# A hybrid encoder layer on one core: the DMA queue in the list scheduler's order, some products later, and fourteen products of a zero operand

## The chip, the cores and the metric

The kernel runs on one core of a Trainium2 chip. The metric is the device time of one execution in microseconds (us); runs of one kernel are summed up by their median. The engines of the core are TensorE (PE in the profile; its weight loads are PEld), VectorE (DVE), ScalarE (ACT), GpSimd (POOL) and SyncE (SP). All DMAs of this kernel are issued from SP's queue, one after the other.

## The reference, cut to what matters

One step of one layer, for 1024 frames of a new stream (prompt) and 32 frames of a running one (sample), with a width of 1024:

```python
h = rmsnorm(x, g_norm)
z = h @ w_in                      # 1024 x 8192: q, k, v of attention, q, k, v, gate of retention, two branch gates
o_a = DiffAttn(h)                 # 8 heads, two softmax maps each: p0 - lam * p1, chunk-causal; then rmsnorm
o_r = Retention(h)                # 8 heads, rotary, decay, a state carried from chunk to chunk; rmsnorm, swish gate
x = x + (sigmoid(g_a) * o_a + sigmoid(g_r) * o_r) @ w_o
x = x + (silu(rmsnorm(x) @ w_ff_gate) * (rmsnorm(x) @ w_ff_up)) @ w_ff_down      # 2816 wide
x = x + sigmoid(rmsnorm(x) @ w_ple_gate) * (p @ w_ple)
```

The sample's 32 frames attend to a cache of 512 keys and values. The new keys and values and the retention states are outputs too.

## The kernel before, in words

Every float32 operand of a large product is scaled and split into two 16-bit halves, and a product is made of three 16-bit ones (high by high, high by low, low by high). So each weight block is loaded in float32 into one of two staging buffers (1 MB each), squared and summed for its scale, and split by ScalarE (high half) and VectorE (low half).

**First stage (`stream`).** The frames are 9 tiles: 8 of 128 prompt frames and one of the 32 sample frames. For each of 8 heads, the tiles are projected one after the other (`project`, L860 to L862, and L871 for the sample tile), once for the attention columns (`unit_a`) and four steps later for the retention and gate columns (`unit_b`). The sample tile's projection is computed the other way around and brought back by `fold` (L878 to L889): ScalarE and VectorE add two parts into `suz`, and TensorE transposes it four times (L887). `attend` computes the scores (L1003 to L1006), the two exponentials, their weighted difference and its two halves (L1051); a DMA transposes the probabilities (L1056, `aT<-p`), and TensorE multiplies them with the values (L1064 to L1068). DMA transposes also bring q and k (L1193, L1195) and the mixed output (L1357) into the layout that TensorE needs; each is issued on SP. Around the last head come the mixed output's way back from memory (`last_mix`, L1464), the splits of `w_o`, the first output products for 352 frames (`wo_rows`, whose products are at L521 to L523) and the load of feed-forward block 0 (`load_gu(0)`, L566).

At the very start, `const_g` multiplies the norm gains onto all partitions (L706), `norm_x` normalizes a tile of x and transposes it on TensorE (L834), and `load_block_steps` loads and splits the first two weight blocks; `weight_scale` sums their squares over the partitions with one product (L336).

**Second stage (`stream_bc`).** The remaining output products, the feed-forward norm (`residual`, whose loads are L1706 and L1708), and 22 blocks of gate and up weights (`load_gu`, its scale's product in `weight_scale`, L336), each used by seven products of half the depth, in `gu_pair`. Then come the down products and the gated embedding, which no list orders.

**What sets the order.** A planner, `Flow`, runs Python generators. Each `yield` names an engine and an estimated time in us (`S`, `V`, `G`, `M` for ScalarE, VectorE, GpSimd and TensorE, `DM` and `X` for the one DMA queue, which it calls D), or a buffer to get and put, an event to wait for, or a delay. At each step it takes the generator that can start first, by its estimates and priorities, and the code behind that `yield` emits the instructions. For a load of 1 MB it estimates 2.9 us of D, for a transpose about 1.2 us, and a landing of 1.3 us and a little more (`landed`). A store is emitted some time after its data is there by the estimate: `store(..., 2.0)` for keys and values, `1.0` for the mixed output.

The instructions of the engines named in `manual_schedule` stay in the order in which they were emitted. Before, these are TensorE, VectorE, ScalarE and GpSimd; SP is not among them, and its DMAs are put in order by the framework's own scheduler:

```python
        with tc.manual_schedule(engines={mybir.EngineType.PE, mybir.EngineType.DVE, mybir.EngineType.Activation,
                                         mybir.EngineType.Pool}):
            flow.add(stream(), 3)
            flow.run()
```

An engine takes its instructions strictly in that order; one that waits holds all behind it.

## Time and profile before

| what | value |
|---|---|
| time, median of 3 runs | 1838.11 us (1836.81 to 1839.48) |
| the profiled execution's own time | 1843.89 us |
| its span, from the first to the last instruction | 1842.0 us |
| mean granted TensorE clock | 0.993 |
| bytes moved by DMA | 180.98 MB, 98 GB/s on the mean |
| DMA transposes issued | 4 x 72 |

In the profile, L12 is line 12 of the kernel. A group is written as line, engine, operation, output <- inputs. A row of the timeline has its start and duration in us from the span's start, and in brackets how long the engine was idle before it and what ended that. A row of windows has the stretch, its length, the busy time of each engine with its instructions, the granted TensorE clock (1.00 is full), the DMA engines' busy share and the rate in GB/s. A row of waits has the total in us, how often, and the longest.

### The profile page before, as it was taken

The numbers are of one execution on the slowest core, as the hardware profiler recorded it, in microseconds if no ns is written. First come the engines' busy times: TensorE is split into PE (matmuls) and PEld (weight loads), VectorE is DVE, ScalarE is ACT, GpSimd is POOL, SyncE is SP. The second block draws the span as 40 slices with busy tenths as digits, with TensorE's granted clock in tenths as the row PEclk, the third lists the DMA queues.
The fourth block names the chain that finished last, engine by engine and source line by source line (L and its number), as shares of the span: only waits on it lengthen the run. The fifth ranks groups of instructions, "written<-read, shape, count | busy, mean of one in ns | idle before, by whom it ended". The sixth has DMA issues, their size and how long they took to land. (4 is left out here: it accounts for less than half of the span.)

```text
span 1842.0 us, 37081 instructions
## 1 busy us (share of the span) xinstructions
PE 1793.9 (97%) x13391; PEld 1154.5 (63%) x13391; DVE 1455.6 (79%) x3881; ACT 1063.9 (58%) x2750; POOL 617.3 (34%) x1038
## 2 busy tenths in 40 slices
PE   7899999999999999999999999999999999999999
PEld 3455555555555555555556867777777766666666
DVE  7888788788787887878886889999999967544553
ACT  7677777677777777777554445655555522102421
POOL 3654546454554655545530002323232100000110
PEclk9999999999999999999999999999999999999999
DMA  6354433445444444434357203221211163121111
GB/s 201 104 125 102 114 86 98 100 104 112 90 109 109 101 123 87 125 82 121 84 155 239 91 5 105 82 93 59 70 47 57 45 263 104 69 78 47 51 48 44
DMA packets 235563, 180.98 MB, mean 98 GB/s; under 512 B 187345, under 2 KB 217553, under 8 KB 227186
## 3 DMA queue, kind: packets, MB, share of 16 engines
q1 hardware_dynamic: 235378, 178.61, 34.3%
q8 instruction: 105, 1.72, 0.4%
q14 instruction: 80, 0.66, 0.1%
HBM read 112.34 MB, written 27.02 MB: 76 GB/s over the span
## 5 line engine op out<-in xcount | busy, mean ns | idle before, releaser
L860 PE MATMUL pj<-w,xh 128*128 128x512 f16 x1024 | 390.3, 381 | 3.1 <-ACT w L512 1.7
L861 PE MATMUL pj<-w,xh 128*128 128x512 f16 x1024 | 390.2, 381 | 0.8 <-DVE w L514 0.8
L862 PE MATMUL pj<-w,xh 128*128 128x512 f16 x1024 | 390.0, 381 | 0.0
L521 PE MATMUL ps<-xh,w 128*128 128x352 f16 (+1 forms) x1000 | 272.9, 278 | 2.2 <-DVE xr L1432 1.9
L523 PE MATMUL ps<-xh,w 128*128 128x352 f16 (+1 forms) x1000 | 272.8, 278 | 1.4 <-DVE w L549 1.4
L522 PE MATMUL ps<-xh,w 128*128 128x352 f16 (+1 forms) x1000 | 272.8, 278 | 0.9 <-DVE xh L1597 0.9
L523 PEld LDWEIGHTS <-w 128*128 128x128 f16 x1632 | 160.2, 98 | 54.1 <-issue 5.4
L521 PEld LDWEIGHTS <-w 128*128 128x128 f16 x1632 | 160.3, 98 | 48.8 <-issue 1.5
L522 PEld LDWEIGHTS <-w 128*128 128x128 f16 x1632 | 160.2, 98 | 48.8 <-issue 2.3
L862 PEld LDWEIGHTS <-xh 128*128 128x128 f16 x1024 | 100.5, 98 | 123.4 <-issue 3.8
L860 PEld LDWEIGHTS <-xh 128*128 128x128 f16 x1024 | 101.0, 99 | 89.2 <-issue 2.2
L861 PEld LDWEIGHTS <-xh 128*128 128x128 f16 x1024 | 100.6, 98 | 85.3 <-issue 4.0
L558 POOL TENSOR_TENSOR st<-st 128x512 f32<-128x512 f32 x54 | 72.0, 1334 | 237.3 <-DVE w L549 174.2
L522 PE MATMUL ps<-tT,w 128*128 128x352 f16 (+1 forms) x504 | 137.3, 277 | 3.2 <-DVE tT L1597 3.2
L523 PE MATMUL ps<-tT,w 128*128 128x352 f16 (+1 forms) x504 | 137.3, 277 | 0.0
L521 PE MATMUL ps<-tT,w 128*128 128x352 f16 (+1 forms) x504 | 137.3, 277 | 0.0
L1023 ACT ACTIVATE p<-sc,nb,scs 128x256 f32<-128x256 f32 (+7 forms) x128 | 106.1, 830 | 50.4 <-DVE nb L1015 37.2
L549 DVE SCALAR_TENSOR_TENSOR w<-st,gus,w 128x512 f16<-128x512 f32 x126 | 128.2, 1020 | 0.1
L1013 DVE TENSOR_REDUCE nm<-sc 128x1 f32<-128x640 f32 (+6 forms) x112 | 102.8, 918 | 25.8 <-PE sc L1006 24.2
L1573 PE MATMUL ps<-a,w 128*128 128x352 f16 x312 | 97.5, 313 | 0.5 <-DVE w L1778 0.5
L1572 PE MATMUL ps<-a,w 128*128 128x352 f16 x312 | 97.5, 312 | 0.0
L1571 PE MATMUL ps<-a,w 128*128 128x352 f16 x312 | 97.5, 312 | 0.0
(439 smaller groups left out, 4588.5 us busy)
## 6 DMA issues: line engine op xcount, KB each, us to landing
st<-in_win_dram SPq DMA_DIRECT2D x30, 1024.0 KB, 5.3
st<-in_wgu_dram SPq DMA_DIRECT2D x22, 1024.0 KB, 5.0
st<-in_wdn_dram SPq DMA_DIRECT2D x16, 704.0 KB, 4.1
out_dram<-kv SPq DMA_DIRECT2D x64, 128.0 KB, 1.9
a_d<-a SPq DMA_DIRECT2D x9, 528.0 KB, 2.7
b<-a_d SPq DMA_DIRECT2D x9, 528.0 KB, 6.8
xh<-mix_d SPq DMA_DIRECT2D x6, 704.0 KB, 6.5
x<-x_d SPq DMA_DIRECT2D x8, 528.0 KB, 7.8
```

The lines of the kernel that those rows point to most:

```text
L521: nc.tensor.matmul(out=ps, lhsT=wh, rhs=ah, start=first, stop=False)
L522: nc.tensor.matmul(out=ps, lhsT=wh, rhs=al, start=False, stop=False)
L523: nc.tensor.matmul(out=ps, lhsT=wl, rhs=ah, start=False, stop=last)
L549: nc.vector.scalar_tensor_tensor(out=w[:, i, 1], in0=src, scalar=s, in1=w[:, i, 0], op0=ALU.mult, op1=ALU.subtract)
L860: nc.tensor.matmul(out=ps, lhsT=xhi, rhs=w[:, k, 0], start=(k == 0), stop=False)
L861: nc.tensor.matmul(out=ps, lhsT=xhi, rhs=w[:, k, 1], start=False, stop=False)
L862: nc.tensor.matmul(out=ps, lhsT=xh[:, k, 1, t0:t0 + P], rhs=w[:, k, 0], start=False, stop=(k == KD - 1))
L1013: nc.vector.tensor_reduce(out=nm[0:R, mc], in_=pv, axis=AX.X, op=ALU.max, negate=True)
L1023: nc.scalar.activation(pt[0:R, 0:NK], ps[0:R, p0:p0 + NK], AF.Exp, bias=nb[0:R, m:m + 1], scale=sc_ap[0:R], accum_out=Z[0:R, m:m + 1])
L1571: nc.tensor.matmul(out=ps, lhsT=wt[:, 0, j], rhs=a[:, 0, cs], start=(first and j == js[0]), stop=False)
L1572: nc.tensor.matmul(out=ps, lhsT=wt[:, 1, j], rhs=a[:, 0, cs], start=False, stop=False)
L1573: nc.tensor.matmul(out=ps, lhsT=wt[:, 2, j], rhs=a[:, 1, cs], start=False, stop=(last and j == js[-1]))
```

## The change

Five things are edited:

- SP is added to the engines of `manual_schedule`, in both stages: its DMAs are now issued in the order in which `Flow` emits them.
- In the last head, `fold` delays its four transposes by 2 us of the planner's time, and `attend` delays the value products of units 5 to 8 by 1.5 us.
- In `load_gu`, the scale's product of blocks 0 to 2 is planned 5.0 us after the sum of squares instead of 3.0.
- A bank of the scores (`idle`) and a zero operand of 16 bits (`zero16`, a view of `suz`, which is zero at the start) are set up, and `busy` issues products of them.
- `busy` is called at three places near the start: 5 products of 512 columns behind the second gain product, 5 behind the scale product of the first weight block, and 4 behind the second group of transposes of the first tile. `Flow` is not told of them.

```diff
-    def weight_scale(amax, n, gi, tag, pool=True, norm=False, total=False, at_bank=None):
+    def weight_scale(amax, n, gi, tag, pool=True, norm=False, total=False, at_bank=None, after=None):
...
             nc.tensor.matmul(out=ps, lhsT=ones16, rhs=amax, start=True, stop=True)
+            if after:
+                after()
...
+    busy_w = [None]
...
-        s, d = yield from weight_scale(am, 1, gi, tag + str(b), tail, norm, norm)
+        s, d = yield from weight_scale(am, 1, gi, tag + str(b), tail, norm, norm, after=busy_w[0] if due == 0 and not b else None)
...
-        yield ("delay", 3.0 if j < 3 else 1.5)
+        yield ("delay", 5.0 if j < 3 else 1.5)
...
+        zero16 = suz[:, 0:2].rearrange("p g c -> p (g c)").bitcast(BF16)
+
+        def busy(pt, n):
+
+            for _ in range(n):
+                nc.tensor.matmul(out=pt, lhsT=mrow, rhs=zero16[:, 0:pt.shape[1]], start=True, stop=True)
...
+        idle = ps_s.tile([P, 1024], F32, tag="sc", name="idle")[:, 0:512]
...
+        busy_w[0] = lambda: busy(idle, 5)
...
                 nc.tensor.matmul(out=pt, lhsT=ones32[0:1], rhs=gb[0:1, js], start=True, stop=True)
+                if j:
+                    busy(idle, 5)
...
                     nc.tensor.transpose(out=pt[:, k], in_=xf[0:R, (4 * b + k) * P:(4 * b + k + 1) * P], identity=id32[0:R, 0:R])
+                if b and not i:
+                    busy(idle, 4)
...
-        def fold(i, ps):
+        def fold(i, ps, late=False):
...
+            if late:
+                yield ("delay", 2)
             yield M(0.5)
...
             yield landed(2 * nb_ * R // 16)
+            if key[0] == H - 1 and i >= NT - 4:
+                yield ("delay", 1.5)
...
-            ps, buf = yield from fold(i, ps)
+            ps, buf = yield from fold(i, ps, h + 1 == H)
...
-                                         mybir.EngineType.Pool}):
+                                         mybir.EngineType.Pool, mybir.EngineType.SP}):
```

The `fold` line stands in `unit_a` and in `unit_b`, and the last one in both stages.

## The prediction

> **What bounds the kernel now.** I read the page first, then TensorE's waits, then windows around each longer wait, then the SP queue's order of time in front of those waits.

> ```profile
> span 1842.0 us, 37081 instructions
> PE 1793.9 (97%) x13391; PEld 1154.5 (63%) x13391; DVE 1455.6 (79%) x3881; ACT 1063.9 (58%) x2750; POOL 617.3 (34%) x1038
> ...
> st<-in_win_dram SPq DMA_DIRECT2D x30, 1024.0 KB, 5.3
> ```

> TensorE (PE) is busy 1793.9 of 1842.0 us, so 48.1 us is all that its idle time can give back, plus what runs at a reduced clock. The load row gives the microseconds from issue to landing of a 1 MB weight block, 5.3. Who TensorE waited for (total, times, longest):

> ```profile
> PE po L1064 <- DMA aT<-p: 13.9, 10, 5.2
> PE pj L887 <- DVE suz L884: 2.6, 1, 2.6
> PE sc L1003 <- DMA kT<-qst: 0.7, 1, 0.7
> PE sc L1003 <- DMA q<-qst: 0.4, 1, 0.4
> ```

> The first row is the product of the probabilities with the values, which waits for the DMA transpose of L1056. With the kT and q transposes, TensorE waits 15.0 us for the one DMA queue, and 2.6 us for the last head's sample rows. A wait is not its whole price, because the clock falls behind it. Windows of waits and of what follows them (length, busy time of PE, PEld, DVE, ACT, POOL, then granted clock):

> ```profile
> 61.57:66.75 5.18, 0.00 (x1) 0.01 (x1) 3.62 (x10) 1.45 (x4) 1.17 (x2) 0.85 1.00 266
> 66.75:72.02 5.27, 5.27 (x24) 2.76 (x25) 3.56 (x14) 3.45 (x14) 3.11 (x7) 0.50 0.33 76
> 328.02:331.43 3.41, 3.41 (x12) 1.49 (x11) 1.56 (x4) 2.05 (x9) 0.79 (x2) 0.50 0.18 39
> 960.50:969.72 9.22, 9.22 (x44) 6.43 (x44) 6.43 (x32) 4.62 (x15) 2.00 (x5) 0.50 0.49 145
> 1120.00:1440.00 320.00, 319.64 (x2860) 246.99 (x2858) 313.95 (x699) 188.06 (x392) 92.89 (x69) 1.00 0.20 71
> ```

> After the idle stretch that ends at 66.75 the clock is 0.50 for 5.27 us, which loses 2.6 us; after the wait at 326.83, 3.41 us (1.7 lost); after that at 960.50, 9.22 us (4.6 lost). The last row is the middle of the feed-forward part: PE 319.64 of 320, so nothing is to be had there, and VectorE (DVE) at 313.95 has 2% left.

> **The change, part by part.** The durations are those of the profiled execution, which took 1843.89 us with its span of 1842.0. The runs' median, 1838.11, is 5.78 lower; I sum against the profiled one and take 5.78 off at the end.

> *The queue's order.* SP's DMAs of the two scheduled stages now stand in the order in which the list scheduler emits them. Nothing is added or removed. None of the list's costs is altered before the last head, so up to there the four compute engines keep their own order and only SP's changes: what can move is where TensorE waits for a DMA, or for an engine that waits for one. The two costliest places show why order matters:

> ```profile
> 54.05 0.74 DVE L514 SCALAR_TENSOR_TENSOR w<-st,B1s,w 128x512 f16<-128x512 f32 x1
> 59.53 0.35 DVE L1051 SCALAR_TENSOR_TENSOR p<-p,lsc 128x128 f16<-128x128 f32 x1
> 59.50 0.34 SPq L427 DMA_DIRECT2D out_dram<-kv  x1
> 59.95 1.13 SPq L454 DMA_DIRECT2D st<-in_win_dram  x1
> 61.17 1.18 SPq L1056 DMA_TRANSPOSE aT<-p  x1
> 66.75 0.29 PE L1064 MATMUL po<-vh,aT 128*128 128x128 f16 x1 [5.18 <-DMA aT<-p]
> ```

> The staging buffer came free at 54.79 (L514 ends), yet its 1 MB load left only at 59.95, because the kv store ahead of it waited for GpSimd (POOL). The transpose, whose data was ready at 59.88, left behind the load, and TensorE got it at 66.75, 5.58 us after its issue. The list adds 2.0 us to a kv store's time and emits a load when its buffer comes free, so I expect the load near 54.8, landed by 60.1 (5.3), and the transpose at about 59.9. A transpose that meets no load took 2.3 us:

> ```profile
> DMA to landing us min/median/max: 2.3/3.2/6.8
> ```

> Landing is then at 62.2 to 63.1, and 0.6 to 1.5 of the 5.18 us are left. At full effect that is 4.1 and the 2.6 us of clock; I take -5.5. Bounds: -7.8 (5.18 and 2.6) and 0 (the load stays in front).

> ```profile
> 316.62 0.81 DVE L1051 SCALAR_TENSOR_TENSOR p<-p,lsc 128x384 f16<-128x384 f32 x1
> 318.72 0.56 SPq L427 DMA_DIRECT2D mix_d<-mixT  x1
> 319.37 0.56 SPq L454 DMA_DIRECT2D st<-in_win_dram  x1
> 320.02 1.29 SPq L1056 DMA_TRANSPOSE aT<-p  x1
> 326.83 0.23 PE L1064 MATMUL po<-vh,aT 128*128 128x128 f16 x1 [2.56 <-DMA aT<-p]
> ```

> Here the data was there at 317.43, and the transpose stood 2.6 us behind a mix store that waited for its own transpose and a 1 MB load. The list gives that store 1.0 us after the landing. Price 2.56 + 1.7 = 4.3; I take -2.5, bounds -4.3 and 0.

> The other waits for transposes in the first stage are 15.0 - 5.18 - 2.56 - 1.29 (the one at 938.61, below) = 6.0 us, in small pieces. I take -2.5, bounds -6.0 and 0.

> What may come in their place is not in this trace. The list charges 2.9 us of the queue for a megabyte that takes 5.3, so transposes will still fall behind loads where the list thinks them clear. I bound it below at 0 and above by 8 us, one more wait of the size at 66.75 with its clock; I take +3.5, nearer to the small waits that make up the 6.0 us.

> *Last units' products later.* The fold's transposes (L887) and the value products of the last head's last four units move behind other work in TensorE's order; the work itself stays.

> ```profile
> 938.61 0.23 PE L1064 MATMUL po<-vh,aT 128*128 128x128 f16 x1 [1.29 <-DMA aT<-p]
> 960.50 1.12 PE L887 MATMUL pj<-cst_sb,suz 128*128 128x128 f32 x4 [2.56 <-DVE suz L884]
> 964.06 0.50 PE L521 MATMUL pj<-xh,w 128*128 128x352 f16 x1
> 999.63 0.31 PE L521 MATMUL ps<-xh,w 128*128 128x352 f16 x1 [1.89 <-DVE xr L1432]
> ```

> The output products (L521 to L523, from 964.06) can stand in front of the fold: 2 us of them fill most of 2.56, and without the idle stretch the 4.6 us at 0.50 go too. From 938.61 the delay of 1.5 us covers 1.29. The most is 1.29 + 2.56 + 4.6 = 8.5. What is late next is the wait at 999.63 for the last residual row on VectorE, which grows if TensorE arrives there sooner; the chain in front of it (weight splits, then feed-forward block 0) has its own pace. I take -6, bounds -8.5 and +2 (the 1.89 doubled).

> *The start of the second stage.* Before, SP fetched later blocks early:

> ```profile
> 987.14 0.60 SPq L566 DMA_DIRECT2D st<-in_wgu_dram  x1
> ...
> 1005.81 0.37 SPq L1708 DMA_DIRECT2D xf<-x_d  x1
> 1008.01 1.04 ACT L579 ACTIVATE wx<-st 128x1024 bf16<-128x1024 f32 x1
> 1018.69 0.17 PE L336 MATMUL mt<-wamh,cst_sb 128*128 128x1 bf16 x1
> ```

> The load at 987.14 is feed-forward block 1, and its squares run at 1008.01. In list order it is emitted after two residual loads, of which the second (L1708) must wait for the first stage's stores, until 1005.81. Block 1 then leaves near 1006 at the latest and lands at 1011 (5.3, as the other blocks of 1 MB), or a few us later behind that 1.4 MB load; its squares wait on ScalarE 3 us or more, and the row sums queue behind them. The scale's product at 1018.69 is what TensorE would wait for; the edit from 3.0 to 5.0 moves it two us back. The residual additions behind ScalarE have the stage's seven PSUM banks as slack before TensorE starves. I take +1; bounds -1.9 (the wait at 999.63, the stage's first, gone) and +7.8 (5.18 and its clock).

> *Fourteen zero products.* The gaps are there, and so is the slow clock:

> ```profile
> 10.76 1.12 PE L834 MATMUL t<-cst_sb,w 128*128 128x128 f32 x4 [2.54 <-DVE w L824]
> 14.30 0.16 PE L336 MATMUL mt<-wamh,cst_sb 128*128 128x1 bf16 x1 [2.42 <-DVE wamh L480]
> 17.14 0.59 PE L860 MATMUL pj<-w,xh 128*128 128x512 f16 x1 [1.72 <-ACT w L512]
> 18.89 0.63 PE L862 MATMUL pj<-w,xh 128*128 128x512 f16 x1
> 24.00 0.50 PE L862 MATMUL pj<-w,xh 128*128 128x512 f16 x1
> 24.98 0.75 DVE L514 SCALAR_TENSOR_TENSOR w<-st,A1s,w 128x512 f16<-128x512 f32 x1
> 25.78 0.38 PE L861 MATMUL pj<-w,xh 128*128 128x512 f16 x1
> ```

> Twelve products start between 18.89 and 24.00, one every 0.43 us, at 0.63 us each; by 25.78 one takes 0.38. At 0.43 the fourteen fill 5 x 0.43 = 2.15 of 2.54, 2.15 of 2.42 and 4 x 0.43 = 1.72 of 1.72 us: they cost nothing, or 0.1 if the last group overruns. But the second half of each product pair (L861) needs VectorE's split of the weights: the last of them ends at 25.73, and TensorE starts on it at 25.78, at full clock already. VectorE sets that pace at either clock, so a fast clock only moves waiting from inside the products to between them. I take 0; bounds +0.3 and -2.6 (the 5.1 us from 18.89 to 24.00, halved).
> [...]

> **Sum.** -5.5 - 2.5 - 2.5 + 3.5 - 6 + 1 + 0 = -12.0. So 1843.89 - 12.0 = 1831.9 under the profiler, and 1826.1 as a median.

> **Rivals.** *All of it goes:* every term at its good end, no new wait: -7.8 - 4.3 - 6.0 - 8.5 - 1.9 - 2.6 = -31.1, or 1807.0. Against it: the list's 2.9 us for a 5.3 us load. *Only the last units gain:* transposes still leave behind loads, new waits take what the old gave, and -5 is left: 1833. For it: thirty 1 MB loads stay in the same queue. *Nothing is left:* the last units' gain runs into the wait at 999.63, which is VectorE's own, and the first stage comes out even: 1838. *Slower:* the queue's head blocks. A store that the list emits before its data exists holds every transpose behind it; for this speaks what the SP queue itself waited for:

> ```profile
> SPq L427 <- POOL kv L1169: 102.1, 36, 7.9
> ```

> The longest stop is 7.9 us, and one that hits TensorE costs 5.18 + 2.6 = 7.8 as at 66.75. With no old wait gone (-6 from the last units alone) one such stop gives 1839.9, two give 1838.1 - 6 + 15.6 = 1847.7: it decides from the second on. Against it: the list's extra 2.0 us for these stores.

> **How the numbers follow.** Chances: forecast 0.50 (own range 1818 to 1833), all of it 0.04, last units only 0.15, nothing 0.12, slower 0.19. Faster by over 0.2%, about what a measurement here can tell (below 1834.4), holds the first two and 0.11 of the third: 0.65. The rest of the third and the fourth: 0.16 within. Slower (above 1841.8): 0.19. The range, 1812 to 1843, leaves out 0.04 below and some 0.13 of the slower case above.

> **What would show it.** Right: no wait at 66.75 and 326.83 and no 0.50 stretch behind them; the 13.9 us row below 8; at 957 to 961 output products in front of the fold, clock 1.00; at the start products of 0.38 us with waits on the L514 splits between them, and the first projection no earlier done. Wrong: kv or mix stores ahead of transposes with longer SP waits, a wait at the scale product of block 1, a longer wait at the second stage's first product, or a first projection that ends 2 us sooner.

## The result and the profile after

The changed kernel takes 1829.14 us (median; 1826.70 to 1831.83), the kernel before 1838.11. The ratio is 0.9949, with a 95% interval of 0.9936 to 0.9963: 0.5% faster. The forecast was 1826.1 in a range of 1812 to 1843.

The profiled execution of the changed kernel took 1831.83 us. Its page begins:

```profile
span 1830.0 us, 37054 instructions
...
PE 1792.6 (98%) x13405; PEld 1154.2 (63%) x13405; DVE 1457.4 (80%) x3883; ACT 1062.4 (58%) x2749; POOL 612.2 (33%) x1037
```

TensorE's work is nearly the same (1792.6 us busy, 1793.9 before) in a span 12.0 us shorter, so it is idle 37.4 us instead of 48.1. The lines of the kernel have moved by 2 to 21: L1064 is now L1085, L1056 is L1075, L1003 is L1022, L887 is L906, L521 is L524, L1432 is L1453, L454 is L457, L427 is L429, L514 is L517, and L860 to L862 are L877 to L879. Who TensorE waited for (total, times, longest):

```profile
PE po L1085 <- DVE orf L1357: 2.2, 1, 2.2
...
PE sc L1022 <- DMA kT<-qst: 2.0, 1, 2.0
...
PE po L1085 <- DMA aT<-p: 0.6, 1, 0.6
```

The row of 13.9 us for aT is down to 0.6. Part of it only changed its name: the 2.2 us put down to `orf` are a wait of L1085, the user of aT, at 86.40 (its transpose, issued at 82.44, lands 3.9 us later), and the 2.0 us for kT are new. The row of `suz` is gone. The place of the wait at 66.75 in the timeline, first SP's issues, then TensorE:

```profile
60.07 1.39 SPq L1075 DMA_TRANSPOSE aT<-p  x1
61.66 1.17 SPq L1214 DMA_TRANSPOSE q<-qst  x1
62.92 0.53 SPq L429 DMA_DIRECT2D out_dram<-kv  x1
63.54 1.19 SPq L1216 DMA_TRANSPOSE kT<-qst  x1
...
68.98 0.66 SPq L457 DMA_DIRECT2D st<-in_win_dram  x1
```

```profile
62.65 0.23 PE L1085 MATMUL po<-vh,aT 128*128 128x128 f16 x1 [0.58 <-DMA aT<-p]
...
64.14 0.40 PE L849 MATMUL t<-cst_sb,w 32*128 32x32 f32 x4 [1.15 <-DVE w L839]
...
67.69 0.37 PE L1022 MATMUL sc<-kT,q 128*128 128x256 f16 x1 [2.04 <-DMA kT<-qst]
```

The transpose is issued at 60.07 and used at 62.65, and of 5.18 us 0.58 are left. But the load did not go ahead to 54.8, as forecast: it went back, to 68.98, behind six other DMAs. And the time saved met two smaller waits at once (64.14 and 67.69). Windows (as in the prediction: length, busy times, granted clock):

```profile
66.99:70.40 3.41, 2.71 (x11) 1.36 (x11) 2.26 (x8) 1.89 (x8) 2.44 (x5) 0.50 0.56 99
87.48:90.89 3.41, 3.41 (x14) 2.06 (x13) 2.35 (x10) 3.41 (x12) 1.19 (x3) 0.50 0.32 105
128.44:131.84 3.40, 3.40 (x24) 2.57 (x23) 3.36 (x7) 1.62 (x4) 0.00 (x0) 0.50 0.72 263
319.00:327.00 8.00, 8.00 (x51) 4.24 (x49) 6.31 (x20) 6.82 (x21) 0.88 (x4) 1.00 0.59 124
```

Behind the waits at 67.69, 86.40 and 128.22 (2.0 to 2.2 us each) the clock is at half for 3.4 us. Of the wait that stood at 326.83 nothing is left, neither wait nor slow clock: TensorE is now some 4.6 us earlier there and is busy for all of 319 to 327 us.

Three points of the trace cut the program into the heads, the tail of the first stage, and the rest: the start of the last projection product (`pj<-w,xh`), the start of the second stage's first product (`ps<-xh,w`), and the end of the span. Lengths in us, worked out from the starts in each trace:

| kernel | heads | tail | rest |
|---|---|---|---|
| before | 954.73 | 44.90 | 842.4 |
| changed | 949.15 | 38.78 | 842.1 |
| changed, another execution | 945.26 | 38.59 | 841.5 |
| before, SP in list order | 945.55 | 43.42 | 843.4 |
| changed, SP not in list order | 953.10 | 38.57 | 840.8 |
| changed, without the delays | 946.85 | 48.06 | 841.7 |
| changed, loads one step earlier | 963.82 | 38.58 | 840.5 |

### The profile page after: what moved, and what is told of

The parts are those of the page before. It is cut to its first block, busy times and chain, and to the rows that moved or that the text cites. A ratio compares the mean times of both kernels' runs of the same rounds, so it can differ in the third digit from the quotient of the medians.

```text
span 1830.0 us, 37054 instructions
## 1 busy us (share of the span) xinstructions
PE 1792.6 (98%) x13405; PEld 1154.2 (63%) x13405; DVE 1457.4 (80%) x3883; ACT 1062.4 (58%) x2749; POOL 612.2 (33%) x1037
## 3 DMA queue, kind: packets, MB, share of 16 engines
q8 instruction: 105, 1.72, 0.4%
## 4 chain that ended last, share of the span: by engine, by line
PE 84%; DVE 7%; DMA 2%; ACT 2%; POOL 2%; issue 2%; SPq 0%; ACTq 0%; POOLq 0%; DVEq 0%
PE ps L524 10%; PE ps L526 10%; PE ps L525 10%; PE pj L877 10%; PE pj L879 10%; PE pj L878 10%; PE ps L1594 4%; PE ps L1593 4%; PE ps L1592 4%; PE sc L1022 2%; PE sc L1025 2%; PE pj L888 1%; DMA st<-in_win_dram 1%; PE po L1085 1%; PE pr L1291 1%
## 5 line engine op out<-in xcount | busy, mean ns | idle before, releaser
L877 PE MATMUL pj<-w,xh 128*128 128x512 f16 x1024 | 389.4, 380 | 2.7 <-ACT w L515 1.3
L879 PE MATMUL pj<-w,xh 128*128 128x512 f16 x1024 | 389.2, 380 | 0.0
L524 PE MATMUL ps<-xh,w 128*128 128x352 f16 (+1 forms) x1000 | 272.8, 278 | 1.8 <-DVE xr L1453 1.5
L525 PEld LDWEIGHTS <-w 128*128 128x128 f16 x1632 | 159.9, 98 | 48.1 <-issue 2.1
L524 PEld LDWEIGHTS <-w 128*128 128x128 f16 x1632 | 160.1, 98 | 47.6 <-ACT w L549 0.7
L879 PEld LDWEIGHTS <-xh 128*128 128x128 f16 x1024 | 100.4, 98 | 124.6 <-issue 4.8
L877 PEld LDWEIGHTS <-xh 128*128 128x128 f16 x1024 | 100.9, 99 | 89.5 <-issue 2.5
L524 PE MATMUL ps<-tT,w 128*128 128x352 f16 (+1 forms) x504 | 137.3, 277 | 0.0
## 6 DMA issues: line engine op xcount, KB each, us to landing
st<-in_win_dram SPq DMA_DIRECT2D x30, 1024.0 KB, 5.6
st<-in_wgu_dram SPq DMA_DIRECT2D x22, 1024.0 KB, 4.9
```

The lines of the kernel that those rows point to most:

```text
L524: nc.tensor.matmul(out=ps, lhsT=wh, rhs=ah, start=first, stop=False)
L525: nc.tensor.matmul(out=ps, lhsT=wh, rhs=al, start=False, stop=False)
L877: nc.tensor.matmul(out=ps, lhsT=xhi, rhs=w[:, k, 0], start=(k == 0), stop=False)
L879: nc.tensor.matmul(out=ps, lhsT=xh[:, k, 1, t0:t0 + P], rhs=w[:, k, 0], start=False, stop=(k == KD - 1))
```

## The experiments: which part brings it

**SP alone, and all but SP.**

```diff
 # e1: the kernel before, in both stages
-                                         mybir.EngineType.Pool}):
+                                         mybir.EngineType.Pool, mybir.EngineType.SP}):
 # e2: the changed kernel, in both stages
-                                         mybir.EngineType.Pool, mybir.EngineType.SP}):
+                                         mybir.EngineType.Pool}):
```

> The kernel before with SP in the list's order in both stages, and nothing else; the four compute engines keep their order to the last instruction. Theory A (the queue's order carries the first stage, where the profile after is 7.2 us ahead when the last head's tail begins): about 1831 us, 7 less than before, with no wait of 5 us at 62 to 67 us. Theory B (the delays of the last units and of the scale products carry the gain): 1837 to 1840. Theory C (the zero products carry it): 1838. A wait at the start of the second stage, where block 1 of the feed-forward now loads late and its product is not planned later, would add 1 to 5 us to each.

> The changed kernel with SP left to the framework's scheduler; the four compute engines stay in the changed kernel's order. Theory A: the first stage keeps its waits, and only the tail's 4.5 us (from 7.2 to 11.7 us ahead in the profile) is left: about 1834 us. Theory B: about 1829. Theory C: 1829 to 1835, with the difference to before there from 25 us on.

| beside before at 1839.12 | median, us | ratio, 95% interval |
|---|---|---|
| SP in list order alone | 1833.95 | 0.9970 (0.9960 to 0.9980) |
| all but SP | 1836.42 | 0.9982 (0.9973 to 0.9991) |
| the whole change again (below) | 1827.97 | 0.9940 (0.9928 to 0.9953) |

So -5.2 and -2.7 alone, less than was expected (about -7 and -4.5), and -11.1 together. That this is 3 us more than the sum is not clear of the noise: by the ratios it is 5.5 and 3.3 us against 11.0, each known to about 2 us. Rows of TensorE's waits, first of the kernel with SP alone, then of the one with all but SP:

```profile
PE po L1064 <- DMA aT<-p: 4.1, 5, 1.3
...
PE pj L887 <- DVE suz L884: 2.6, 1, 2.6
```

```profile
PE po L1085 <- DMA aT<-p: 12.1, 8, 4.9
```

SP's order alone takes the aT row to 4.1 and leaves the fold's 2.6; all but SP leaves the aT row at 12.1, with the 4.87 us wait at 66.30, and has no fold row. With SP alone the other four engines run the same instructions in the same order as before, to the last one. The two causes are in two places, and the table of lengths says the same: the heads are 9.2 us shorter with SP alone and 1.6 without it, the tail 1.5 and 6.3. The lengths don't add up either: the two spans are 9.6 and 9.5 us shorter, the changed kernel's 12.0 and 16.7 in its two executions. All are taken against the one profile of before, which lies 5.78 above its median.

**Without the zero products, and the same kernel again.**

```diff
 # e3: the changed kernel; e4 is the changed kernel as it is
-        busy_w[0] = lambda: busy(idle, 5)
+        busy_w[0] = None
...
-                    busy(idle, 5)
+                    pass
...
-                if b and not i:
-                    busy(idle, 4)
```

> The changed kernel without its fourteen zero products. Theory A with VectorE setting the pace of the first projection: the same as the changed kernel within 0.5 us, with products of 0.63 us up to about 24 us and the first projection ended at the same time. Theory C (the clock granted earlier is worth what half speed costs there): 2.6 us slower, and that at 26 us already.

> The changed kernel itself, to compare the others with on one chip: 1829 us, 9 less than before. If the clock's drops behind waits fall by chance, its profile shows other drops than the first did, at the same waits.

Without them 1828.59 (0.9942, 0.9930 to 0.9954), with them 1827.97: nothing that can be told apart. The timelines of TensorE, first with them, then without:

```profile
8.19 2.31 PE L667 MATMUL idle<-suz,mrow 128*128 128x512 bf16 x5
...
11.85 1.49 PE L667 MATMUL idle<-suz,mrow 128*128 128x512 bf16 x5
...
18.41 0.38 PE L878 MATMUL pj<-w,xh 128*128 128x512 f16 x1 [0.99 <-DVE w L517]
...
25.68 0.38 PE L878 MATMUL pj<-w,xh 128*128 128x512 f16 x1 [0.28 <-DVE w L517]
```

```profile
25.66 0.38 PE L876 MATMUL pj<-w,xh 128*128 128x512 f16 x1 [0.28 <-DVE w L517]
```

The second five zero products take 1.49 us where the first five took 2.31, and the projection's product at 18.41 takes 0.38 instead of 0.63: the clock is full there. It did not last: after two more waits, of 1.32 and 0.99 us at 17.05 and 18.41, it is at half from 19.20 to 22.62. In the other execution of the same kernel (e4) it is full from 17.1 on. Windows of the first and the second:

```profile
19.20:22.62 3.42, 2.88 (x9) 0.84 (x7) 3.42 (x8) 3.42 (x6) 2.00 (x2) 0.50 0.07 12
17.10:25.70 8.60, 5.34 (x23) 2.31 (x23) 8.60 (x18) 6.17 (x11) 3.39 (x4) 1.00 0.47 167
```

Yet the product that stood at 25.78 before stands at 25.68 and 25.74 in these two, and at 25.66 without the zero products, each time behind VectorE's split.

**Is it VectorE's split that sets the pace?** If so, zero products must pay once the split is short. Here each step of the first two weight blocks makes the low halves of 32 columns instead of 256 and leaves the others out.

```diff
 # e11: the changed kernel; e12: the same without the zero products
+            c2 = slice(256 * b, 256 * b + 32) if due == 0 else cs
-            nc.vector.scalar_tensor_tensor(out=w[:, ks, 1, cs], in0=st[:, ks], ...
+            nc.vector.scalar_tensor_tensor(out=w[:, ks, 1, c2], in0=st[:, ks, 0:c2.stop - c2.start], ...
```

> The changed kernel with the low-half split on VectorE of the first two weight blocks cut from 256 columns to 32 in each step, so that the low halves of those weights are left unset in the other columns; all else stays. Theory (VectorE's splits set the pace of the first projection): with the zero products the clock is full from 12.4 us and TensorE no longer waits for the splits, so the first projection's last product of the high-by-low pairs, 0.10 us earlier than before in the changed kernel (25.68), comes at 22 to 24 us. Rival (something else in front, the high-half split on ScalarE or the load, sets the pace): 25 us or later.

> The same cut of the first low-half splits, without the fourteen zero products. Theory: TensorE's half clock now sets the pace of the first projection (0.43 us per product until about 24 us), so its last product comes 1 to 3 us later than in the run with the zero products and the same cut; this is where zero products would pay. Rival: within 0.5 us of that run, so that the zero products pay nowhere at this start.

The twentieth projection product, the one at 25.78 before, is at 23.42 in the first timeline and at 24.71 in the second (their line numbers are one higher, and one lower, than in the changed kernel):

```profile
19.30 0.38 PE L878 MATMUL pj<-w,xh 128*128 128x512 f16 x1 [1.07 <-ACT w L515]
...
23.42 0.38 PE L879 MATMUL pj<-w,xh 128*128 128x512 f16 x1
```

```profile
22.39 0.63 PE L876 MATMUL pj<-w,xh 128*128 128x512 f16 x1
...
24.71 0.38 PE L877 MATMUL pj<-w,xh 128*128 128x512 f16 x1
```

The short split brings 2.3 us with the zero products (from 25.68) and 0.95 without (from 25.66), where products still take 0.63 at 22.39; so the zero products are now worth 1.3 us (with them every projection product from 16.55 to 29.65 takes 0.38). The theory holds at its lower end. Of my bound of 2.6 us half comes out; with them ScalarE's high halves are next in line, a wait of 1.07 us at 19.30. The whole times, 1828.72 and 1829.20, can't tell 1 us apart.

**Without the two delays of the last head.**

```diff
 # e5: the changed kernel
-                yield ("delay", 2)
+                yield ("delay", 0)
...
-                yield ("delay", 1.5)
+                yield ("delay", 0.0)
```

> The changed kernel with the two delays of the last head (2 us at the fold, 1.5 us at the value products) taken out. If they carry the tail: the wait for the fold's sum of about 2.6 us is back near 950 us, with or without a clock drop behind it (up to 4.6 us), and 1.3 us at the value products: 2.5 to 7 us slower than the changed kernel, 1831 to 1835. If the wait for the residual row at the start of the second stage swallows it: within 1 us, 1828 to 1829, and a shorter wait there.

1837.39 us, ratio to before 0.9984 (0.9975 to 0.9993): 8 to 9 us of the gain gone, more than my term of 6 for them. TensorE and VectorE:

```profile
952.64 0.66 PE L906 MATMUL pj<-cst_sb,suz 128*128 128x128 f32 x4 [2.57 <-DVE suz L901]
...
994.91 0.45 PE L524 MATMUL ps<-xh,w 128*128 128x352 f16 x1 [8.05 <-DVE xr L1453]
```

```profile
987.84 0.58 DVE L1453 SCALAR_TENSOR_TENSOR xr<-pj,o1d,xr 128x352 f32<-128x352 f32 x1 [6.39 <-DMA xr<-in_xT_dram]
...
994.29 0.58 DVE L1453 SCALAR_TENSOR_TENSOR xr<-pj,o1d,xr 128x352 f32<-128x352 f32 x1
```

The fold's wait is back. From the last projection product to the first output product it is 8.86 us instead of 6.87, so 2.0 us. The other 7.3 us come at the second stage's first product: VectorE is idle 6.39 us for a residual load, holds its weight splits behind it, and reaches the last residual row only at 994.29. The load was issued at 980.30 here and at 978.12 in the changed kernel.

The load alone is not the reason. The kernel with SP alone has no delays either, and issues this load at 979.20; but there VectorE does the splits (L549) first, and the residual row (L1432) then waits for nothing:

```profile
980.37 2.07 DVE L549 SCALAR_TENSOR_TENSOR w<-st,gus,w 128x512 f16<-128x512 f32 x3
...
983.62 0.57 DVE L1432 SCALAR_TENSOR_TENSOR xr<-pj,o0d,xr 128x352 f32<-128x352 f32 x1
```

Up to 975.9 us TensorE's order in these two kernels is the same, zero products aside. The first thing that differs is the scale's product of feed-forward block 0, which the 5.0 us of `load_gu` put later, and with it the splits. The tail is 43.42 us with SP alone and 48.06 here: of the 9.3 us that this run is above the changed kernel's 38.78, 4.6 are what the edit from 3.0 to 5.0 costs while the delays are missing, and 4.7 are the delays' own, 2.0 of them at the fold. Here two parts of the change depend on each other.

## The experiments: the queue's order

**The load in front of the transposes.** Each 1 MB load is emitted one step earlier, ahead of the planner's wait for the queue.

```diff
 # e9: the changed kernel
-            yield DM(1.0)
             (the load)
+            yield DM(1.0)
```

> The changed kernel, but each 1 MB load of the first stage's weights is emitted one step earlier, as soon as its buffer is free and ahead of the planner's wait for the DMA queue; only SP's order changes. Theory (the wait at 66.75 went because in list order the load stands behind the transposes): loads stand in front of transposes again, one or more waits of 3 us or more for aT, kT or q come back between 60 and 100 us and in the later heads, and the time is 2 to 10 us above the changed kernel's 1828 to 1829. Rival (a transpose behind a load costs nothing, since the units have slack, as they had for the kv stores): within 1.5 us of the changed kernel, no wait above 2.5 us for a transpose.

1843.18 us beside 1829.02 for the kernel of e10, below, on the same chip: 14 us slower, and slower than before (ratio 1.0017, 1.0007 to 1.0027). All of it is in the heads (963.82 in the table, tail and rest as in the changed kernel), and the four other engines keep the changed kernel's order to the last instruction. The theory holds, and its 2 to 10 us were too few. The places were not the ones I named first: around 62 us the queue's order is unchanged, and the long waits come in the later heads. Waits, then SP and TensorE at the longest:

```profile
PE sc L1022 <- DMA kT<-qst: 11.0, 6, 4.9
```

```profile
865.72 0.57 SPq L456 DMA_DIRECT2D st<-in_wo_dram  x1
866.34 1.56 SPq L1216 DMA_TRANSPOSE kT<-qst  x1
```

```profile
874.93 0.48 PE L1022 MATMUL sc<-kT,q 128*128 128x384 f16 x1 [4.88 <-DMA kT<-qst]
```

The transpose behind the load landed 8.5 us after its issue at 866.34, and was used 7.0 us after the issue ended at 867.90. In the changed kernel that load stands behind kT and aT, kT lands 2.4 us after its issue, and TensorE is busy for all of 855 to 876 us:

```profile
856.95 1.26 SPq L1216 DMA_TRANSPOSE kT<-qst  x1
858.30 1.22 SPq L1075 DMA_TRANSPOSE aT<-p  x1
...
861.45 0.60 SPq L457 DMA_DIRECT2D st<-in_wo_dram  x1
```

```profile
855.00:876.00 21.00, 21.00 (x169) 12.46 (x165) 19.59 (x69) 13.65 (x47) 13.28 (x25) 1.00 0.46 114
```

**The queue's head.** The slower rival was a store emitted before its data exists; the reason against it was the list's extra 2.0 us for these stores. Here they are emitted without it:

```diff
 # e7: the changed kernel
-            flow.add(store(kvo[h, t0:t0 + RT], kv[0:RT], "kv", 2.0))
+            nc.sync.dma_start(out=kvo[h, t0:t0 + RT], in_=kv[0:RT]); flow.add(store(None, None, "kv", 2.0))
```

> The changed kernel with each store of keys and values emitted at the list's time of its data instead of 2.0 us and more later; the engines keep their order. If those 2 us keep the queue's head free: SP waits longer for GpSimd's kv than the changed kernel does, transposes leave later, and TensorE waits for them again in the first stage: 3 to 8 us slower, 1831 to 1836. If the stores' place is of no matter, since the transposes have slack in TensorE's order: within 1 us of 1828.

SP's wait for GpSimd is back, at nearly the size of before (102.1; in the changed kernel it is 8.0):

```profile
SPq L1191 <- POOL kv L1190: 94.4, 35, 7.0
...
PE po L1085 <- DMA aT<-p: 2.4, 2, 1.2
```

TensorE does not notice: 1827.45 us (0.9928, 0.9915 to 0.9940), if anything the fastest. My reason against the rival was wrong. Here a kv store stopped the head of the queue for up to 7.0 us, and the transposes behind it still came in time. What did cost time, in the run with the loads one step earlier, was 1 MB of transfer in front of them, and not at every load: there, five waits of TensorE for a kT or an aT (0.6 to 4.9 us) have a load next ahead of the transpose or one DMA further.

**An honest price of the load.** The planner charges 2.9 us for a megabyte that takes 5.3.

```diff
 # e8: the changed kernel
-    return {"D": mb * 2.9}
+    return {"D": mb * 5.3}
```

> The changed kernel with the list's cost of a megabyte at 5.3 us of the queue instead of 2.9, as the trace has it. All engines' orders move with it. If the list's too short loads leave transposes waiting (about 1 to 2 us each at 67 and 85 us): those waits go, 2 to 4 us faster, 1824 to 1826. If the list now spreads the loads too thin and weight blocks come late: slower, over 1830, with waits of TensorE for splits of w.

1857.97 us, ratio 1.0095 (1.0079 to 1.0110): 29 us slower than the changed kernel. It says little on single transposes, since the planner orders all engines by it from the first load on. The largest waits of TensorE on another engine are now those for a normalized tile of x (8.8 us in four waits, the longest 4.9), which neither of my two theories had named. In this planner 2.9 works better than the measured time; why, this run does not show.

**The second stage.** The scale's product at 3.0 again, and SP in list order in the first stage only:

```diff
 # e6: the changed kernel
-        yield ("delay", 5.0 if j < 3 else 1.5)
+        yield ("delay", 3.0 if j < 3 else 1.5)
 # e10: the changed kernel, second stage
-                                             mybir.EngineType.Pool, mybir.EngineType.SP}):
+                                             mybir.EngineType.Pool}):
```

> The changed kernel with the scale products of blocks 0 to 2 planned at 3.0 us again. The kernel with SP alone in the list's order showed a wait of 1.41 us at that product of block 0, and 0.37 before: that wait comes back, 1 to 1.5 us slower than the changed kernel without a clock drop, up to 5 with one; 1829 to 1833. The rival, that the chain of block 0 on VectorE sets the second stage's start anyway: same as the changed kernel.

> The changed kernel with SP in list order in the first stage only; in the second stage the framework orders SP's DMAs, as before. Theory (the second stage's order of SP is worth nothing, since the traces agree to 0.3 us from its start to its end): within 1.5 us of the changed kernel, 1827 to 1830, and the wait at the second stage's first product stays between 1 and 2.5 us. Rival (my +1 term: block 1's load late in list order costs TensorE a little): 1 to 3 us faster than the changed kernel.

1828.79 (0.9939, 0.9926 to 0.9951) and 1829.02 (0.9944, 0.9930 to 0.9958): both are the changed kernel's time. With the delays in, neither edit does anything that can be measured; without them the 5.0 us cost time, as the run without the delays shows. The rows of the changed kernel, SP, ScalarE and TensorE, show the cover:

```profile
992.75 0.38 SPq L569 DMA_DIRECT2D st<-in_wgu_dram  x1
```

```profile
1001.00 1.06 ACT L582 ACTIVATE wx<-st 128x1024 bf16<-128x1024 f32 x1 [4.59 <-DMA st<-in_wgu_dram]
```

```profile
987.93 0.31 PE L524 MATMUL ps<-xh,w 128*128 128x352 f16 x1 [1.51 <-DVE xr L1453]
...
1010.58 0.17 PE L336 MATMUL mt<-wamh,cst_sb 128*128 128x1 bf16 x1
```

Block 1 is fetched late, as forecast, and ScalarE waits 4.59 us for it, but the scale's product at 1010.58 finds its data there, and TensorE is busy for all 23.0 us from 988 to 1011.

## Why the prediction was right, and where it was off

- **The sum.** Under the profiler -12.0 was forecast, to 1831.9, and 1831.83 came. That it fits to 0.1 us is luck: this execution is the slowest of five, and the other profile of the same kernel took 1827.08. As a median it is 1829.14 instead of 1826.1, a gain of 9.0. The 3 us are in one term: I took off 5.78, by which the profiled execution of before lay above its median. The changed kernel's lay only 2.69 above its own. The likely reason is that a part of the 5.78 was slow clock of that one execution, which I had already priced in the terms. Two traces point that way: with SP alone the same wait at the fold (2.56 us) is followed by 3.41 us at 0.50 where it was 9.22 before, and with all but SP the wait that was at 326.83 (there 1.94 us, at 325.36) is followed by full clock (the mean clock of that execution is 0.997, of before's 0.993). There is no second profile of the kernel before to settle it.
- **The wait at 66.75** (-5.5) **and the new waits** (+3.5). Together -2.0. At the 145th projection product the gain is 3.3 us (it starts at 64.47, before at 67.74). At the 209th it is -0.3 (90.65 and 90.36): the waits at 67.69 and 86.40 with the clock behind them took all of it. The one at 86.40 is of the kind that I had expected: its transpose (issued at 82.44) stands next behind a 1 MB load (78.94). In the other execution of the same kernel 2.0 are left there (88.40). The mechanism is as forecast, for a load behind the transposes instead of ahead of them; the ahead (54.8) was wrong. Why the list comes to the load so late no run shows. The planner's wait for the queue is not the reason, since a step earlier (e9) the load leaves at 68.36, behind the same six DMAs.
- **The wait at 326.83** (-2.5). From the 801st to the 1001st projection product (272 to 335 us before) the gain grows by 5.5 us in both executions, from 0.9 behind to 4.6 ahead and from 2.8 to 8.3 ahead. This term was mis-sized: of a price of 4.3 I took about half, and all of it came, with some small waits nearby, and nothing in its place. Not all of it is the queue's order: with all but SP the same stretch is 2.5 us shorter than before, with the wait still there but at full clock. So about 3.0 are the order's, and the rest is mostly slow clock of the profiled execution.
- **The other transposes' waits** (-2.5). From 335 us to the last projection 1.0 and 1.2 us came in the two executions, 2.7 with SP alone. For all heads -7.0 was forecast; -5.6 and -9.5 were measured.
- **The last units** (-6). The tail is 6.1 and 6.3 us shorter, and as short without SP in the list (38.57): the delays do it, at the size forecast. A part of that size is again slow clock in the profile of before: with SP in the list and 3.0 us in `load_gu`, the tail is 43.42 without the delays and 38.59 with them (e6), 4.8 us. The picture was wrong. The output products don't stand in front of the fold:

```profile
952.60 0.38 PE L322 MATMUL mt<-o0mc,cst_sb 1*128 1x1 f32 x2 [1.12 <-DVE o0mc L314]
...
953.72 0.60 PE L906 MATMUL pj<-cst_sb,suz 128*128 128x128 f32 x4
...
956.02 0.31 PE L524 MATMUL pj<-xh,w 128*128 128x352 f16 x1
```

  The norm's and the retention's small products fill the place, with a wait of 1.12 left, and the fold takes 0.60 us instead of 1.12, at full clock. The idle time is no longer in one piece, and the 9.22 us at 0.50 are gone:

```profile
951.00:960.00 9.00, 7.35 (x68) 5.58 (x65) 7.76 (x29) 5.04 (x18) 2.31 (x5) 1.00 0.82 231
```

- **The start of the second stage** (+1). It is 0: the wait there is 1.51 instead of 1.89, and the rest of the program is 0.3 to 0.9 us shorter. A cover held, as I had said; that it is the PSUM banks behind ScalarE no run separates. The edit from 3.0 to 5.0, to which I gave two us, is worth nothing beside the delays and costs 4.6 us without them.
- **Fourteen zero products** (0). Right, and for the reason given: VectorE's split sets the pace. With them the clock was full earlier (the second five took 1.49 us where the first took 2.31, and the projection's product at 18.41 took 0.38 where before's took 0.63 at 18.89), but of my bound of 2.6 us nothing came: the product behind the last split stands at 25.68 with them and at 25.66 without. With the split out of the way 1.3 us came.
- **The slower rival** (0.19). Its mechanism is harmless for the kv stores, as the run without their 2.0 us shows (1827.45 us, with stops of up to 7.0). But the side on which it stood is real, by another way: one step in the emission of the loads makes this very change slower than before (1843.18). What makes this order good is where it puts the loads, and I had weighed the stores.

## What to carry to other kernels

In a DMA queue with large loads and small latency-bound transfers, look first at which large load stands directly ahead of a transfer that TensorE waits for; here stores that stopped the queue for up to 7.0 us were harmless (1827.45 us) where 1 MB ahead was not (1843.18). Before filling idle time to raise the clock, find who sets the pace of the products behind it: here the same products were worth nothing behind VectorE's split (25.68 us with them, 25.66 without) and 1.3 us once it was short. When a sum is made against one profiled execution, the difference to the median is a term of its own and not a constant.

## What was not expected of the hardware

The clock does not always fall behind the same wait. In the changed kernel a wait for ScalarE is followed by 3.40 us at 0.50 (the window from 128.44, above). The same wait in its timeline, then in another execution's, and the window behind that:

```profile
128.22 0.40 PE L1022 MATMUL sc<-kT,q 128*128 128x512 f16 x1 [1.97 <-ACT p L1042]
```

```profile
126.21 0.38 PE L1022 MATMUL sc<-kT,q 128*128 128x512 f16 x1 [1.94 <-ACT p L1042]
```

```profile
126.50:130.00 3.50, 3.50 (x35) 2.54 (x34) 3.46 (x7) 2.53 (x7) 0.23 (x1) 1.00 0.65 234
```

1.97 and 1.94 us, half clock and full. The two profiles differ by 4.7 us in span (1825.3 and 1830.0) and by 0.997 to 0.994 in the mean clock. So a wait of about 2 us can carry a price in one execution and none in the next.

```profile
125.02:128.43 3.41, 1.44 (x7) 0.57 (x6) 2.98 (x13) 1.73 (x4) 1.53 (x4) 1.00 0.96 201
122.96:126.37 3.41, 1.47 (x8) 0.59 (x6) 2.97 (x13) 1.68 (x4) 1.54 (x4) 1.00 0.95 214
```

Both waits lie inside one window, in which TensorE was busy for 0.42 and 0.43 of it; the clock falls behind the first and stays full behind the second. The kernel before has the same wait, 1.96 us up to 128.17. There a border of the grid, at 126.63, cuts it in two, and the clock stays full:

```profile
123.21:126.63 3.42, 3.00 (x16) 1.39 (x15) 3.16 (x8) 1.10 (x6) 2.96 (x8) 1.00 0.83 108
126.63:130.04 3.41, 1.87 (x23) 1.39 (x23) 3.17 (x12) 2.44 (x7) 0.00 (x0) 1.00 0.27 62
130.04:133.45 3.41, 3.41 (x24) 2.11 (x22) 2.97 (x8) 3.36 (x7) 1.26 (x2) 1.00 0.12 27
```

In the traces of before and of the changed kernel the full clock fell behind ten windows of the grid. In six of them TensorE was busy for 0.00 to 0.40 of the window, and no window with so little kept the clock; in the other four it was busy for 0.42 to 0.54. With shares like these the clock also stayed full: behind 0.42, 0.45 and 0.50 before (windows from 1836.71, 997.03 and 1109.67), 0.50 in the changed kernel's (from 1097.82), and the 0.43 of the other execution above. What decides there no run shows.

Four of the ten windows lie in the first 130 us of the changed kernel's execution, and in them TensorE was idle for 1.9 to 2.2 of 3.41 us.
